# Eight conditioning vectors: row sums by VectorE with a 32x32 transpose, then selection matmuls for a group of vectors

## The chip, the core and the metric

The kernel runs on one core of one Trainium2 chip. The core has a matrix engine (TensorE, PE in the profile, with its weight loads as PEld), a vector engine (VectorE, DVE), a scalar engine (ScalarE, ACT), GpSimd (POOL) and SyncE (SP), which here only starts DMA transfers. Each engine works through its own instructions in order and waits for the others by semaphores. All of them read and write SBUF, 128 partitions wide; TensorE writes its results to PSUM. The metric is the time of one launch on the device in microseconds (us), lower is better.

## The reference

The program is a two-layer encoder trunk over 1024 tokens of width 1024, all in f32. Layer 0 has a short gated convolution and an MLP with squared ReLU (width 4096); then one shared key and value side is computed; layer 1 has latent attention with 8 heads and a second MLP. Each norm is followed by a shift and a scale which come from one conditioning vector c:

```python
mod = silu(c) @ ada_w[l] + ada_b[l]                  # 1024 -> 6 * 1024
sh_m, sc_m, g_m, sh_f, sc_f, g_f = split(mod, 6)
h = rmsnorm(x, g) * (1 + sc) + sh                    # and the like for the shared side, with kv_ada_w
```

So for each of these vectors 1024 numbers are wanted, and each is a sum over the 1024 rows of a 1024x1024 block of `ada_w`. Eight of them are wanted as columns ("feature major": the feature on the partition, 128 features x 8 columns), and they are what the change is about.

## The kernel before, in words

Almost all of the time goes into large matrix products. Each f32 factor is split into a high and a low part of a reduced format, `split_w` (L162): ScalarE writes the high part (L163), VectorE the difference (L164). `mm` (L156) then issues three matmuls for each product (L160). The larger products are done by a scheme with seven products for eight, so that VectorE also forms sums of operands.

**The vectors.** `ada_acc` (L171) computes one vector up to its last sum. It holds `acc`, 128x1024, in one buffer. For each of eight blocks k of 128 rows, SP loads 512 KB of weights into `raw` (one of four buffers, started at L115), and VectorE adds the block, multiplied row by row with silu(c): L188 for the first, L190 for the others. After eight blocks `acc[p, f]` holds 128 partial sums for each feature f, one on each partition, and they still have to be added over the partitions. `ada_fm` (L198) does this for the vectors that are wanted as columns: its `end` issues eight matmuls (L208), in each of which a 128x128 block of `acc` is the weight and a column of ones the right side, so that 128 features come out as one column. VectorE then adds the bias (L210) and, for a scale, adds one and multiplies with the norm's gain (L212, L213). `ada_bc` (L218) does something like it for vectors that are wanted on every partition (L233); it is not changed.

**Where the vectors are computed.** Both functions return lists of ten steps: the start, eight blocks, the end. The steps are appended to one list `bg`, and `run_bg(n)` (L241) takes n of them from its front at fixed places between the large products. In the conv phase that is three at a time after each pair of products, nine times, and then whatever is left (L987, L996). In the down projection of layer 0 (`down_pairs`) it is one or two with each block of weights (L709) and the rest at the end (L717). In attention it is five with each head (L1361). So the vectors s0f and h0f (the MLP of layer 0) are computed in the conv phase; s1m, h1m, skv and hkv (layer 1 and the shared side) in the down projection; s1f and h1f (the MLP of layer 1) in attention.

**What sets the order.** The instructions are put into the engines' queues by a scheduler, which goes by its own costs and by which buffers are free; only regions marked `pinned` keep the order of the program. Tiles of one tag share a fixed number of buffers, and pools are given places in SBUF one after another. Where two pools share the same space, the first use of the second waits for the last use of the first. `up` (the operands of the pairs in the conv phase, `uphi` and `uplo`) and the pools of the conv projection before it are such pools.

Of the kernel before, what the change touches and what calls it, by code (L numbers as in the profile page):

```python
# [8 lines left out]
F32 = mybir.dt.float32  # L9
# [3 lines left out]
ALU = mybir.AluOpType  # L13
AX = mybir.AxisListType
# [3 lines left out]
P = 128  # L18
D = 1024
S = 1024  # L20
KD = D // P
# [18 lines left out]
RMS = math.sqrt(D)  # L40
# [9 lines left out]
def trunk_kernel(ctx: ExitStack, tc: tile.TileContext, x, c, ada_w, ada_b, norm_g, conv_in_w, conv_w,  # L50
                 conv_b, conv_out_w, kv_ada_w, kv_ada_b, kv_norm_g, kv_a_w, kv_a_norm_g, kv_b_w,
                 q_a_w, q_a_norm_g, q_b_w, attn_o_w, mlp_up_w, mlp_down_w, consts, out):
    nc = tc.nc
    uid = [0]

    def nm(s):
        uid[0] += 1
        return f"{s}_{uid[0]}"

    def pool(name, side="left", **kw):  # L60
        return tc.alloc_tile_pool(name=name, bufs=1, side=side, reuse_waits="tile", **kw)

    cp = pool("cp")
    rawp = pool("rawp")
    ad = pool("ad")
# [25 lines left out]
    def raw_tile():  # L91
        return rawp.tile([P, D], F32, tag="raw", name=nm("raw"), bufs=4)
# [4 lines left out]
    def row_tile():  # L97
        return yp.tile([P, D], F32, tag="y", name=nm("y"), bufs=NT)
# [15 lines left out]
    def ld(out_, in_):  # L114
        nc.sync.dma_start(out_, in_)  # L115
# [3 lines left out]
    ident = cs[:, C_ID:C_ID + P]  # L119
# [21 lines left out]
    ones = cp.tile([P, P], F32, name="ones")  # L141
# [5 lines left out]
    vecs = cp.tile([P, VEC_ROWS], F32, name="vecs")  # L147
    bias = cp.tile([P, BIAS_ROWS], F32, name="bias")

    def gain(l, v):  # L150
        return vecs[:, (l * 4 + v) * 8:(l * 4 + v) * 8 + 8]

    V_CW, V_CB, V_KV, V_QA, V_KA = 64, 88, 96, 104, 107
# [17 lines left out]
    def ada_acc(accp, w, col, bias_row=None):  # L171

        acc = accp.tile([P, D], F32, tag="acc", name=nm("acc"), bufs=1)
        raws = {}
        if bias_row is not None:
            nc.gpsimd.memset(acc, 0.0)
            ld(acc[0:1, :], bias_row)

        def load(k):
            raws[k] = raw_tile()  # L180
            ld(raws[k], w[k * P:(k + 1) * P, col:col + D])

        def one(k):
            if k + 1 < KD:
                load(k + 1)
            raw, s = raws[k], csil[:, k:k + 1]
            if k == 0 and bias_row is None:
                nc.vector.tensor_scalar(acc, raw, s, None, op0=ALU.mult)  # L188
            else:
                nc.vector.scalar_tensor_tensor(acc, raw, s, acc, op0=ALU.mult, op1=ALU.add)  # L190

        load(0)
        return acc, [lambda k=k: one(k) for k in range(KD)]

    vtile = {}
    spare = [mm_ps]

    def ada_fm(accp, key, w, col, brow, g=None):  # L198

        st = {}  # L200

        def begin():
            st["acc"], st["t"] = ada_acc(accp, w, col)

        def end():
            p_ = spare[0]()
            for k in range(KD):
                nc.tensor.matmul(p_[:, k:k + 1], st["acc"][:, k * P:(k + 1) * P], ones[:, 0:1], start=True, stop=True)  # L208
            v = cp.tile([P, KD], F32, name=nm("v"))
            nc.vector.tensor_tensor(v, p_[:, :KD], bias[:, brow:brow + KD], op=ALU.add)  # L210
            if g is not None:
                nc.vector.tensor_scalar(v, v, 1.0, RMS, op0=ALU.add, op1=ALU.mult)  # L212
                nc.vector.tensor_tensor(v, v, g, op=ALU.mult)  # L213
            vtile[key] = v

        return [begin] + [lambda k=k: st["t"][k]() for k in range(KD)] + [end]

    def ada_bc(accp, key, w, col, brow, grow):  # L218

        st = {}  # L220

        def begin():
            v = accp.tile([P, D], F32, tag="gmb", name=nm("gmb"), bufs=1)
            ld(v, grow.partition_broadcast(P))
            st["v"] = v
            st["acc"], st["t"] = ada_acc(accp, w, col, brow)

        def end():
            v = st["v"]
            for n in range(2):  # L230
                sl = slice(n * HALF, (n + 1) * HALF)
                p_ = mm_ps()
                nc.tensor.matmul(p_, ones, st["acc"][:, sl], start=True, stop=True)  # L233
                nc.vector.scalar_tensor_tensor(v[:, sl], p_, RMS, v[:, sl], op0=ALU.mult, op1=ALU.mult)
            vtile[key] = v

        return [begin] + [lambda k=k: st["t"][k]() for k in range(KD)] + [end]

    bg = []
# [153 lines left out]
    def h_steps(tp, ys, half, key, dst):  # L393

        hi, lo = dst
        s1, sh = vtile["s" + key], vtile["h" + key]
        tts = {}

        def step(k):
            p_ = tp_ps()  # L400
            for t in range(4):
                nc.tensor.transpose(p_[:, t * P:(t + 1) * P], ys[half * 4 + t][:, k * P:(k + 1) * P], ident)
            tt = tp.tile([P, HALF], F32, tag="tt", name=nm("tt"), bufs=2)
            nc.scalar.activation(tt, p_, AF.Identity, scale=s1[:, k:k + 1], bias=sh[:, k:k + 1])
            tts[k] = tt

        def split(k):
            nc.vector.tensor_copy(hi[:, k, :], tts[k])
            nc.vector.tensor_tensor(lo[:, k, :], tts[k], hi[:, k, :].bitcast(F32), op=ALU.subtract)

        return [(lambda k=k: step(k), lambda k=k: split(k)) for k in range(KD)]
# [355 lines left out]
    w0, w1 = ada_w[0], ada_w[1]  # L767
# [233 lines left out]
    nx = pool("nx", "right")  # L1001
    ar = []
    bg += ada_bc(ad, "g0m", w0, 2 * D, ada_b[0:1, 2 * D:3 * D], norm_g[0, 1:2, :])
    bg += ada_fm(ad, "s0f", w0, 4 * D, 32, gain(0, 2))
    bg += ada_fm(ad, "h0f", w0, 3 * D, 24)
    conv_phase()

    def down_phase(slots, sizes, wd, src_fn, g, xsrc, xdst, next_w, key, ys=None, pairs=True):
# [82 lines left out]
    bg += ada_bc(ad, "g0f", w0, 5 * D, ada_b[0:1, 5 * D:6 * D], norm_g[0, 3:4, :])  # L1091
    last = mlp_up(0, up, hs, firsts, 2)
    ys = [row_tile() for _ in range(NT)]
    bg += ada_fm(ad, "s1m", w1, 1 * D, 48 + 8, gain(1, 0))
    bg += ada_fm(ad, "h1m", w1, 0 * D, 48)
    bg += ada_fm(ad, "skv", kv_ada_w, D, 96 + 8, vecs[:, V_KV:V_KV + 8])
    bg += ada_fm(ad, "hkv", kv_ada_w, 0, 96)
    ar, slots = down_pairs(ys, mlp_down_w[0], last)
    banks(False)
    up, ws, hs, firsts, ys = down_phase(slots, (2, 2, 4), mlp_down_w[0], from_dram(hd), "g0f", xs[0], xs[1], q_a_w[0], "1m", ys=ys,  # L1100
# [83 lines left out]
    steps = h_steps(tp, ys, 0, "kv", hk[0])  # L1184
# [3 lines left out]
    steps = h_steps(tp, ys, 1, "kv", hk[1])  # L1188
# [18 lines left out]
    ld(stab, consts[:, C_T + S:])  # L1207
    at = pool("at", "right")
    bg += ada_bc(ad, "g1m", w1, 2 * D, ada_b[1:2, 2 * D:3 * D], norm_g[1, 1:2, :])
    bg += ada_fm(ad, "s1f", w1, 4 * D, 48 + 32, gain(1, 2))  # L1210
    bg += ada_fm(ad, "h1f", w1, 3 * D, 48 + 24)

    def part(pl, tag, bufs, shape):
        return tuple(pl.tile(shape, F32R, tag=tag + "hl"[i], name=nm(tag), bufs=bufs) for i in range(2))
# [277 lines left out]
```

## Time and profile before

| what | value |
|---|---|
| median of 3 runs | 2186.09 us (2185.59 to 2193.38) |
| the profiled execution's span | 2186.4 us |
| TensorE busy | 2101.2 us (96%) |
| VectorE busy | 1523.9 us (70%) |
| ScalarE busy | 1052.9 us (48%) |
| GpSimd busy | 4.0 us |
| granted TensorE clock, mean | 0.991 |

The profile shows one execution; no other time is given for it than its span, from the first to the last instruction. A row of a timeline begins with the start and the duration in us, then the engine, the line of the kernel, the operation, the output and inputs by name, the shapes and how many instructions the row holds; in brackets stands how long the engine had been idle before and what released it. A group row has the busy time and the mean duration in ns behind the first bar, and the idle time before it with its releaser behind the second. A row of waits has us in total, how often, and the longest. A row of windows has the busy time of each engine in that stretch, then the granted TensorE clock, the share of DMA and GB/s.

### The profile page before, as it was taken

What the parts mean: (1) busy time and instruction counts of PE and PEld (TensorE: products, weight loads), DVE (VectorE), ACT (ScalarE), POOL (GpSimd) and SP (SyncE); (2) the same over time, 40 slices, a digit from 0 to 9 for tenths busy, and PEclk for the clock granted to TensorE, in tenths of its full rate; (3) what the DMA queues carried; (4) which work ended last, traced back from release to release, by engine and by line L of the source; (5) the groups of instructions that cost most, each with busy time, mean ns of one, the idle gap of its engine ahead of it and who ended that gap; (6) DMA issues with size and microseconds to landing.
All of it is one profiled execution on the core that took longest, in us unless ns stands there. A gap on an engine that the chain in (4) does not pass through costs nothing.

```text
span 2186.4 us, 25316 instructions
## 1 busy us (share of the span) xinstructions
PE 2101.2 (96%) x9702; PEld 1728.0 (79%) x9702; DVE 1523.9 (70%) x2001; ACT 1052.9 (48%) x1501; POOL 4.0 (0%) x8
## 2 busy tenths in 40 slices
PE   4999999899999999999899999999899999999998
PEld 3778888678888788888777888878688887888886
DVE  6777766876565679776788776665865655566665
ACT  4533354744454444344665555564645444444422
POOL 0000000000000000000000000000000000000000
PEclk9999999999999999999999999999999999999999
DMA  7435464256443985554224231053254544853343
GB/s 226 132 119 152 130 205 139 78 166 194 155 159 117 339 291 189 167 170 143 77 63 125 68 112 44 30 171 128 66 171 155 179 165 149 301 174 97 123 137 116
DMA packets 233551, 323.61 MB, mean 148 GB/s; under 512 B 18165, under 2 KB 141394, under 8 KB 233430
## 3 DMA queue, kind: packets, MB, share of 16 engines
q1 hardware_dynamic: 198424, 244.11, 35.8%
q10 hardware_dynamic: 35006, 77.89, 9.4%
q8 instruction: 76, 1.25, 0.3%
q14 instruction: 45, 0.37, 0.1%
HBM read 244.35 MB, written 77.59 MB: 147 GB/s over the span
## 4 chain that ended last, share of the span: by engine, by line
PE 78%; DVE 12%; ACT 6%; DMA 2%; issue 2%; ACTq 0%; SPq 0%; DVEq 0%
PE one L160 39%; PE mm L160 19%; PE big L160 9%; PE tp L160 6%; ACT junk L249 2%; PE big L1285 2%; DVE y L306 2%; DVE raw L307 2%; PE tp L1311 1%; DVE y L300 1%; DVE acc L190 1%; DVE small L1288 1%; DMA raw<-in_ada_w_dram 1%; DMA aw<-in_ada_w_dram 1%; ACT small L251 1%
## 5 line engine op out<-in xcount | busy, mean ns | idle before, releaser
L160 PE MATMUL one<-slot,uphi 128*128 128x512 f32 x1224 | 378.3, 390 | 0.0
L160 PE MATMUL big<-slot 128*128 128x512 f32 x1536 | 353.0, 390 | 0.5 <-DVE slot L164 0.4
L160 PEld LDWEIGHTS big<-slot 128*128 128x128 f32 x1536 | 287.7, 188 | 60.0 <-DVE slot L164 0.9
L160 PEld LDWEIGHTS one<-slot,uphi 128*128 128x128 f32 x1224 | 230.7, 188 | 48.4 <-issue 0.5
L160 PE MATMUL one<-slot,uplo 128*128 128x512 f32 x612 | 240.9, 394 | 8.1 <-ACT y L568 2.3
L164 DVE TENSOR_TENSOR uplo<-raw,uphi 128x1024 fp32r<-128x1024 f32 x127 | 153.1, 1221 | 133.9 <-ACT uphi L163 133.8
L160 PE MATMUL one<-ring,ring 128*128 128x512 f32 x864 | 197.9, 390 | 3.6 <-DVE ring L164 3.6
L163 ACT ACTIVATE ring<-w 128x1024 fp32r<-128x1024 f32 x84 | 88.9, 1059 | 225.6 <-PE tp L160 117.6
L163 ACT ACTIVATE uphi<-raw 128x1024 fp32r<-128x1024 f32 x127 | 134.5, 1061 | 121.6 <-PE one L160 89.1
L160 PEld LDWEIGHTS one<-ring,ring 128*128 128x128 f32 x864 | 161.7, 188 | 38.7 <-ACT ring L163 3.1
L160 PE MATMUL mm<-slot,uphi 128*128 128x512 f32 x520 | 166.6, 401 | 9.5 <-DVE slot L367 9.3
L164 DVE TENSOR_TENSOR ring<-w,ring 128x1024 fp32r<-128x1024 f32 x84 | 102.7, 1222 | 87.9 <-ACT ring L163 86.1
L160 PEld LDWEIGHTS one<-slot,uplo 128*128 128x128 f32 x612 | 115.5, 189 | 35.4 <-ACT y L493 3.3
L160 PE MATMUL mm<-ring,ring 128*128 128x512 f32 x576 | 139.5, 390 | 0.0
L160 PE MATMUL tp<-ring,ring 128*128 128x512 f32 x576 | 138.7, 389 | 0.0
L190 DVE SCALAR_TENSOR_TENSOR acc<-raw,csil,acc 128x1024 f32<-128x1024 f32 x88 | 112.8, 1282 | 32.3 <-DMA raw<-in_ada_w_dram 30.0
L160 PEld LDWEIGHTS mm<-ring,ring 128*128 128x128 f32 x576 | 107.6, 188 | 23.5 <-issue 0.8
L160 PEld LDWEIGHTS tp<-ring,ring 128*128 128x128 f32 x576 | 108.1, 188 | 22.4
L160 PEld LDWEIGHTS mm<-slot,uphi 128*128 128x128 f32 x520 | 98.9, 192 | 32.8 <-DVE slot L367 10.8
L493 ACT ACTIVATE y<-one 128x512 f32<-128x512 f32 x66 | 39.0, 591 | 163.4 <-PE one L160 102.2
L160 PE MATMUL one<-slot,s 128*128 128x512 f32 x468 | 112.6, 389 | 0.0
L164 DVE TENSOR_TENSOR ring<-raw,ring 128x1024 fp32r<-128x1024 f32 x84 | 102.4, 1219 | 11.8 <-ACT ring L163 11.8
(255 smaller groups left out, 3515.8 us busy)
## 6 DMA issues: line engine op xcount, KB each, us to landing
ha<-y ACTq DMA_DIRECT2D x168, 256.0 KB, 4.2
raw<-ha SPq DMA_DIRECT2D x84, 512.0 KB, 4.1
raw<-in_ada_w_dram SPq DMA_DIRECT2D x80, 512.0 KB, 3.9
raw<-in_mlp_up_w_dram SPq DMA_DIRECT2D x70, 512.0 KB, 4.2
w<-in_mlp_down_w_dram SPq DMA_DIRECT2D x48, 512.0 KB, 6.3
raw<-hd SPq DMA_DIRECT2D x32, 512.0 KB, 4.4
hd<-y ACTq DMA_DIRECT2D x24, 512.0 KB, 3.7
xs<-raw ACTq DMA_DIRECT2D x24, 512.0 KB, 3.0
```

What stands on the lines that cost most here:

```text
L160: nc.tensor.matmul(out_, lhs[a], rhs[b], start=first and i == 0, stop=last and i == 2, skip_group_check=more)
L163: nc.scalar.activation(hi, src, AF.Copy)
L164: nc.vector.tensor_tensor(lo, src, hi.bitcast(F32), op=ALU.subtract)
L190: nc.vector.scalar_tensor_tensor(acc, raw, s, acc, op0=ALU.mult, op1=ALU.add)
L249: nc.scalar.activation(junk, src, AF.Square, accum_out=ss)
L251: nc.scalar.activation(rt, ss, AF.Sqrt, bias=eps_d)
L300: nc.vector.tensor_tensor(y, y, p_, op=ALU.add)
L306: nc.vector.scalar_tensor_tensor(y, y, rroot(ss), self.gmb, op0=ALU.mult, op1=ALU.mult)
L307: nc.vector.tensor_tensor(xr, xr, y, op=ALU.add)
L493: nc.scalar.activation(dst, x_, AF.Copy)
L1285: nc.tensor.matmul(o_, a, m_, start=j == 0, stop=j == 4 and b * HALF + w < n)
L1288: nc.vector.tensor_reduce(mx, sp[:, :n], AX.X, ALU.max, negate=True)
```

## The change

VectorE adds over 32 columns where TensorE added over all 128 rows. `reduce` reads `acc`, 128x1024, as 32 blocks of 32 columns. With `apply_transpose` each 32x32 square (32 partitions by 32 columns) is transposed and then summed, so that `part[p, i, b]` holds, for the partition 32g + r, the sum over the 32 partitions of quadrant g of feature 32b + r. What is left is to add the four quadrants and to bring the 32 features of each block to their place among 128. Both are done by a matmul with a 0/1 matrix `sel`: `sel[:, b, :]` puts row r of each quadrant into row 32b + r. Four such matmuls, one for each b, accumulate in PSUM, and one set of four serves all vectors of a group: 16 columns for the two vectors of the conv phase, 32 for the four of the down projection, 16 for the two of attention. The operations on the bias and the gain are the same as before, but those of a group now come together.

`sel` is made once, by GpSimd, as a step of the list `bg`. A vector still has ten steps (the last is now the sum), and each group has one step more, its `end`; with `selectors` the list of the conv phase is two steps longer, the other two lists are one longer. The last part of the diff lowers the space that is kept in each partition for the descriptors of dynamic DMAs from 16384 bytes to 256; the new tiles take 3200 bytes of it.

```diff
--- before.py
+++ after.py
@@ -195,25 +195,53 @@
     vtile = {}
     spare = [mm_ps]
 
-    def ada_fm(accp, key, w, col, brow, g=None):
-
-        st = {}
-
-        def begin():
-            st["acc"], st["t"] = ada_acc(accp, w, col)
+    sel = cp.tile([P, 4, P], F32, name="sel")
+
+    def selectors():
+
+        stacked = cp.tile([P, 32], F32, name="stacked")
+        nc.gpsimd.memset(sel, 0.0)
+        nc.gpsimd.tensor_copy(stacked, ident[:, 0:32])
+        for g in range(1, 4):
+            nc.gpsimd.tensor_tensor(stacked, stacked, ident[:, 32 * g:32 * g + 32], op=ALU.add)
+        for b in range(4):
+            nc.gpsimd.tensor_copy(sel[:, b, 32 * b:32 * b + 32], stacked)
+
+    def ada_fm(accp, vectors):
+
+        n = len(vectors)
+        part = cp.tile([P, n, 32], F32, name=nm("part"))
+        steps = []
+
+        def one(i, key, w, col, brow, g):
+            st = {}
+
+            def begin():
+                st["acc"], st["t"] = ada_acc(accp, w, col)
+
+            def reduce():
+                nc.vector.tensor_reduce(part[:, i, :], st["acc"].rearrange("p (b i) -> p b i", i=32), AX.X, ALU.add,
+                                        apply_transpose=True)
+
+            steps.extend([begin] + [lambda k=k: st["t"][k]() for k in range(KD)] + [reduce])
 
         def end():
             p_ = spare[0]()
-            for k in range(KD):
-                nc.tensor.matmul(p_[:, k:k + 1], st["acc"][:, k * P:(k + 1) * P], ones[:, 0:1], start=True, stop=True)
-            v = cp.tile([P, KD], F32, name=nm("v"))
-            nc.vector.tensor_tensor(v, p_[:, :KD], bias[:, brow:brow + KD], op=ALU.add)
-            if g is not None:
-                nc.vector.tensor_scalar(v, v, 1.0, RMS, op0=ALU.add, op1=ALU.mult)
-                nc.vector.tensor_tensor(v, v, g, op=ALU.mult)
-            vtile[key] = v
-
-        return [begin] + [lambda k=k: st["t"][k]() for k in range(KD)] + [end]
+            blocks = part.rearrange("p v (k b) -> p b v k", b=4)
+            for b in range(4):
+                nc.tensor.matmul(p_[:, :n * KD].rearrange("p (v k) -> p v k", k=KD), sel[:, b, :], blocks[:, b], start=b == 0,
+                                 stop=b == 3)
+            for i, (key, w, col, brow, g) in enumerate(vectors):
+                v = cp.tile([P, KD], F32, name=nm("v"))
+                nc.vector.tensor_tensor(v, p_[:, i * KD:(i + 1) * KD], bias[:, brow:brow + KD], op=ALU.add)
+                if g is not None:
+                    nc.vector.tensor_scalar(v, v, 1.0, RMS, op0=ALU.add, op1=ALU.mult)
+                    nc.vector.tensor_tensor(v, v, g, op=ALU.mult)
+                vtile[key] = v
+
+        for i, vector in enumerate(vectors):
+            one(i, *vector)
+        return steps + [end]
 
     def ada_bc(accp, key, w, col, brow, grow):
 
@@ -1001,8 +1029,8 @@
     nx = pool("nx", "right")
     ar = []
     bg += ada_bc(ad, "g0m", w0, 2 * D, ada_b[0:1, 2 * D:3 * D], norm_g[0, 1:2, :])
-    bg += ada_fm(ad, "s0f", w0, 4 * D, 32, gain(0, 2))
-    bg += ada_fm(ad, "h0f", w0, 3 * D, 24)
+    bg.append(selectors)
+    bg += ada_fm(ad, [("s0f", w0, 4 * D, 32, gain(0, 2)), ("h0f", w0, 3 * D, 24, None)])
     conv_phase()
 
     def down_phase(slots, sizes, wd, src_fn, g, xsrc, xdst, next_w, key, ys=None, pairs=True):
@@ -1091,10 +1119,8 @@
     bg += ada_bc(ad, "g0f", w0, 5 * D, ada_b[0:1, 5 * D:6 * D], norm_g[0, 3:4, :])
     last = mlp_up(0, up, hs, firsts, 2)
     ys = [row_tile() for _ in range(NT)]
-    bg += ada_fm(ad, "s1m", w1, 1 * D, 48 + 8, gain(1, 0))
-    bg += ada_fm(ad, "h1m", w1, 0 * D, 48)
-    bg += ada_fm(ad, "skv", kv_ada_w, D, 96 + 8, vecs[:, V_KV:V_KV + 8])
-    bg += ada_fm(ad, "hkv", kv_ada_w, 0, 96)
+    bg += ada_fm(ad, [("s1m", w1, 1 * D, 48 + 8, gain(1, 0)), ("h1m", w1, 0 * D, 48, None),
+                      ("skv", kv_ada_w, D, 96 + 8, vecs[:, V_KV:V_KV + 8]), ("hkv", kv_ada_w, 0, 96, None)])
     ar, slots = down_pairs(ys, mlp_down_w[0], last)
     banks(False)
     up, ws, hs, firsts, ys = down_phase(slots, (2, 2, 4), mlp_down_w[0], from_dram(hd), "g0f", xs[0], xs[1], q_a_w[0], "1m", ys=ys,
@@ -1207,8 +1233,7 @@
     ld(stab, consts[:, C_T + S:])
     at = pool("at", "right")
     bg += ada_bc(ad, "g1m", w1, 2 * D, ada_b[1:2, 2 * D:3 * D], norm_g[1, 1:2, :])
-    bg += ada_fm(ad, "s1f", w1, 4 * D, 48 + 32, gain(1, 2))
-    bg += ada_fm(ad, "h1f", w1, 3 * D, 48 + 24)
+    bg += ada_fm(ad, [("s1f", w1, 4 * D, 48 + 32, gain(1, 2)), ("h1f", w1, 3 * D, 48 + 24, None)])
 
     def part(pl, tag, bufs, shape):
         return tuple(pl.tile(shape, F32R, tag=tag + "hl"[i], name=nm(tag), bufs=bufs) for i in range(2))
@@ -1476,7 +1501,7 @@
     from concourse import mybir as _mybir
     from concourse.bass_utils import run_bass_kernel_spmd as _run
 
-    nc = _bacc.Bacc("TRN2", target_bir_lowering=False, num_devices=1)
+    nc = _bacc.Bacc("TRN2", target_bir_lowering=False, num_devices=1, dynamic_dma_scratch_size=256)
     arrays, args = {}, []
     for name in _INS + ["consts"]:
         a = _consts() if name == "consts" else _np.ascontiguousarray(inputs[name])
```

Three places show what the scheduler made of it (the numbers in the names and the line numbers are shifted a little in the new program). The first is ScalarE's queue in the conv phase, before: `uphi_1051` is the high part of the first weights of the pairs, `w_950` and `w_974` are splits of conv weights, L895 makes operands of the pairs, L870 and L871 evict the last conv products from PSUM.

```order
L163 ACTIVATE w_950<-w_948 128x384 [waits DMAHW2_49,Activation_49]
L895 ACTIVATE slot_776<-raw_567 128x512 [waits DVE_49]
L895 ACTIVATE q_998<-y_996 128x512 [waits DVE_49]
L163 ACTIVATE w_974<-w_972 128x384 [waits DMAHW3_49,PE_49,Activation_49]
L895 ACTIVATE b_997<-y_996 128x512
L870 ACTIVATE y_1030<-mm_782 128x512 [waits PE_49]
L871 ACTIVATE y_1029<-mm_781 128x512 [waits PE_49]
L870 ACTIVATE y_1030<-one_779 128x512 [waits PE_49]
L871 ACTIVATE y_1029<-one_778 128x512 [waits PE_49]
L163 ACTIVATE uphi_1051<-raw_1045 128x1024 [waits DMAHW6_49,DVE_49,PE_49]
```

And the same queue of the new program, where `uphi_1053` is that split and L923 and L898 are the lines L895 and L870:

```order
L163 ACTIVATE w_850<-w_848 128x384 [waits DMAHW5_49,PE_49,Activation_49]
L163 ACTIVATE uphi_1053<-raw_1047 128x1024 [waits DMAHW6_49]
L923 ACTIVATE slot_777<-raw_449 128x512 [waits DVE_49]
L923 ACTIVATE slot_778<-raw_449 128x512 [waits DVE_49]
L923 ACTIVATE slot_777<-raw_509 128x512 [waits DVE_49]
```

The split has moved up behind the conv weights `w_850`, 21 places, and waits for its DMA alone; before, it stood behind the last evictions and also waited for VectorE and TensorE.

The second place is VectorE's queue at the end of the conv phase, before. `s_352` is the low part of an operand that TensorE's next product reads.

```order
L190 SCALAR_TENSOR_TENSOR acc_1943<-raw_2211,csil,acc_1943 128x1024 [waits DMAHW2_49,DVE_49]
L506 TENSOR_TENSOR y_2050<-y_2050,one_2075 128x512 [waits Activation_49]
L190 SCALAR_TENSOR_TENSOR acc_1943<-raw_2271,csil,acc_1943 128x1024 [waits DMAHW3_49,DVE_49]
L965 TENSOR_TENSOR y_1977<-one_1978,y_1836 128x512 [waits PE_49]
L164 TENSOR_TENSOR uplo_2166<-raw_2104,uphi_2165 128x1024 [waits Activation_49]
L446 TENSOR_TENSOR raw_2104<-raw_2104,raw_2102 128x512 [waits DVE_49]
L484 TENSOR_TENSOR y_2106<-y_2106,mm_2137 128x512 [waits PE_49]
L449 TENSOR_TENSOR raw_2102<-raw_2102,raw_2104 128x512 [waits DVE_49]
L164 TENSOR_TENSOR slot_2307<-raw_2328,slot_2307 128x1024 [waits DMAHW4_49,Activation_49]
L164 TENSOR_TENSOR s_352_2171<-raw_2104,s_351_2170 128x512 [waits Activation_49]
```

And now (L993 is the line L965):

```order
L190 SCALAR_TENSOR_TENSOR acc_2063<-raw_2208,csil,acc_2063 128x1024 [waits DMAHW1_49,DVE_49]
L534 TENSOR_TENSOR y_2047<-y_2047,one_2072 128x512 [waits Activation_49]
L190 SCALAR_TENSOR_TENSOR acc_2063<-raw_2268,csil,acc_2063 128x1024 [waits DMAHW2_49,DVE_49]
L190 SCALAR_TENSOR_TENSOR acc_2063<-raw_2271,csil,acc_2063 128x1024 [waits DMAHW3_49,DVE_49]
L223 TENSOR_REDUCE part_150<-acc_2063 128x32 [waits DVE_49]
L993 TENSOR_TENSOR y_1974<-one_1975,y_1845 128x512 [waits PE_49]
L164 TENSOR_TENSOR uplo_2163<-raw_2101,uphi_2162 128x1024 [waits Activation_49]
L512 TENSOR_TENSOR y_2103<-y_2103,mm_2134 128x512 [waits PE_49]
L474 TENSOR_TENSOR raw_2101<-raw_2101,raw_2099 128x512 [waits DVE_49]
L164 TENSOR_TENSOR slot_2308<-raw_2329,slot_2308 128x1024 [waits DMAHW4_49,Activation_49]
L477 TENSOR_TENSOR raw_2099<-raw_2099,raw_2101 128x512 [waits DVE_49]
L164 TENSOR_TENSOR s_350_2168<-raw_2101,s_349_2167 128x512 [waits Activation_49]
```

One more addition to `acc` stands here, since the list runs one step later, and behind it the sum with its transpose; then the same instructions as before follow.

The third is TensorE's queue there, before and now:

```order
L160 MATMUL one_2075<-q_998,uplo_2037 128x512
L160 MATMUL one_2075<-q_998,uphi_2036 128x512 x2
L208 MATMUL mm_2275<-ones,acc_1943 128x1 [waits DVE_49]
L208 MATMUL mm_2275<-ones,acc_1943 128x1 x7
L160 MATMUL one_2107<-slot_776,s_352_2171 128x512 [waits DVE_49]
L160 MATMUL one_2107<-slot_776,s_351_2170 128x512 [waits Activation_49]
```

```order
L160 MATMUL one_2072<-q_1000,uplo_2034 128x512
L160 MATMUL one_2072<-q_1000,uphi_2033 128x512 x2
L232 MATMUL mm_2276<-part_150,sel 128x16 [waits DVE_49,Pool_49]
L232 MATMUL mm_2276<-part_150,sel 128x16 [waits Pool_49] x3
L160 MATMUL one_2104<-slot_778,s_350_2168 128x512 [waits DVE_49]
L160 MATMUL one_2104<-slot_778,s_349_2167 128x512 [waits Activation_49]
```

The selection matmuls of the group stand at the very place where the eight matmuls of its second vector stood; the group of the first vector, further up, is gone.

## The prediction

> **What bounds the kernel now.** I read the page first: busy shares, the 40 slices and the chain.
>
> ```profile
> span 2186.4 us, 25316 instructions
> PE 2101.2 (96%) x9702; PEld 1728.0 (79%) x9702; DVE 1523.9 (70%) x2001; ACT 1052.9 (48%) x1501; POOL 4.0 (0%) x8
> PE   4999999899999999999899999999899999999998
> ...
> DVE  6777766876565679776788776665865655566665
> ...
> PE 78%; DVE 12%; ACT 6%; DMA 2%; issue 2%; ACTq 0%; SPq 0%; DVEq 0%
> ```
>
> PE works for 2101.2 of 2186.4 us. Only the first slice is far from full, and the chain of waits lies on PE for 78%. So a matmul that goes is worth its whole time wherever PE has no gap, and what VectorE does costs nothing unless it comes late for PE. The span is 2186.4 us, the median of the runs 2186.1, so a difference worked out against the span carries over to the median less 0.3 us.
>
> Next the view of the line that the change removes, L208, with the engine that waited for it, and PE's timeline around one of its eight groups.
>
> ```profile
> L208 PE MATMUL mm<-ones,acc x80: 164/250/250, 245.9 to 1338.3; 128*128 128x1 f32 x80
> L208 PE MATMUL one<-ones,acc x48: 164/250/250, 784.7 to 917.5; 128*128 128x1 f32 x48
> DVE v L210: 10.9, 7
> ```
>
> ```profile
> 784.75 1.84 PE L208 MATMUL one<-ones,acc 128*128 128x1 f32 x16
> 786.45 3.03 PE L160 MATMUL mm<-ring,ring 128*128 128x512 f32 x12
> 789.31 2.88 PE L160 MATMUL tp<-ring,ring 128*128 128x512 f32 x12
> 792.03 2.88 PE L160 MATMUL mm<-ring,ring 128*128 128x512 f32 x12
> ```
>
> The 128 records are 64 matmuls, two passes for each f32 matmul, 16 passes in a group. The group starts at 784.75 and the next work at 786.45: 1.70 us, or 0.106 us a pass, for one column of output. Twelve matmuls of the ring follow each other in 2.72 us (789.31 to 792.03), but the first twelve after the group took 2.86 (786.45 to 789.31), so it also costs 0.14 us of pipeline. **One vector costs 1.84 us of PE**, with nothing else able to run there.
>
> Windows then tell how much slack the other engines have where the groups stand.
>
> ```profile
> core 0: us, PE busy (x) PEld busy (x) DVE busy (x) ACT busy (x) POOL busy (x), PEclk, DMA share, GB/s
> 110.00:150.00 40.00, 37.79 (x160) 30.76 (x159) 27.04 (x32) 15.55 (x21) 0.00 (x0) 0.96 0.38 110
> 250.00:300.00 50.00, 49.31 (x226) 40.78 (x225) 37.51 (x42) 19.09 (x23) 0.00 (x0) 1.00 0.58 182
> 750.00:800.00 50.00, 50.00 (x230) 41.65 (x230) 37.54 (x36) 21.52 (x25) 0.00 (x0) 1.00 0.82 282
> 800.00:850.00 50.00, 50.00 (x230) 41.68 (x229) 45.07 (x41) 19.77 (x22) 0.00 (x0) 1.00 0.76 253
> 850.00:900.00 50.00, 49.96 (x228) 41.11 (x227) 45.89 (x50) 18.98 (x22) 0.00 (x0) 1.00 0.55 178
> 1300.00:1350.00 50.00, 49.47 (x300) 43.37 (x299) 35.63 (x63) 27.77 (x54) 0.00 (x0) 1.00 0.20 67
> ```
>
> PE is full in all of them but the first, where 2.21 us are lost to a stall and (1 − 0.96) × 40 = 1.6 us to a lower granted clock. VectorE is near its own limit from 800 to 900 us.
>
> **Removed: eight groups.** 8 × 1.84 = 14.7 us of PE, two of them in the conv phase, four in the down projection of layer 0 (784.75 and three more up to 917.5), two in attention, where PE is full to 1%.
>
> **Added on PE: three groups of four selection matmuls.** Eight passes a group, of 16 or 32 columns. The trace has passes of one column at 0.106 us and f32 passes of 512 columns, below.
>
> ```profile
> L233 PE MATMUL mm<-acc,ones 128*128 128x512 f32 x16 | 7.8, 598 | 0.0
> L1288 DVE TENSOR_REDUCE small<-big 128x1 f32<-128x1024 f32 x8 | 9.8, 1223 | 3.2 <-PE big L1286 2.8
> L190 DVE SCALAR_TENSOR_TENSOR acc<-raw,csil,acc 128x1024 f32<-128x1024 f32 x88 | 112.8, 1282 | 32.3 <-DMA raw<-in_ada_w_dram 30.0
> L176 POOL MEMSET acc<- 128x1024 f32 x4 | 3.8, 956 | 1545.5 <-DVE lat L1133 734.0 <-DVE uplo L164 712.1 <-DMA raw<-in_ada_w_dram 99.4
> ```
>
> So a group lies between 8 × 0.106 + 0.14 = 1.0 us and 8 × 0.598 + 0.14 = 4.9 us. Sixteen or 32 columns are far nearer to one than to 512, though the right side is read at a stride of four elements; I take 1.0, and 3.0 us for the three. The upper end would be 14.7, the whole saving.
>
> **Added on VectorE: eight sums of 128x1024 into 128x32 with the transpose.** A plain sum of as many elements takes 1.223 us (L1288, from PSUM and with one output a row). With a transpose there is no row. Below I bound it by the plain 1.2, above by one pass for the sum and seven more of the kind, some 10 us; I take 1.22, since an instruction that reads 1024 elements a row takes 1.2 to 1.3 us in both rows here whatever it does with them. Eight are 9.8 us, hidden under PE's matmuls where VectorE has slack. On the other side VectorE no longer stands behind PE for each vector:
>
> ```profile
> DVE v L210 <- PE one L208: 7.8, 3, 4.8
> DVE v L210 <- PE mm L208: 2.3, 1, 2.3
> ```
>
> These are the waits from 735 to 960 us: 10.1 us of VectorE standing idle in its own order, until PE reached a group. The change puts 4 × 1.22 = 4.9 us of sums in that stretch and takes most of the 10.1 out, so I cost it at nothing there; without that cover it would be 4.9. [...]
>
> **Added on POOL: the selection matrix.** One memset of 128x512, half of a 956 ns row, five copies and three additions of small blocks, at the start. POOL's first work of before waits until 99.4 us for a DMA, and PE needs the matrix only just ahead of 284.79 us (quoted further down). Nothing; what it could disturb is VectorE in the first slice, where PE is only four tenths busy; 0 to 2 us, within the range.
>
> **Moved: the stall at the first pair.** The smaller reserve for DMA descriptors frees 12.9 KB of each partition after the new tiles, and in the new order ScalarE's split of the first pair's weights waits for its load alone and stands some 20 rows earlier; in the old order it stands behind the evictions of the conv projection.
>
> ```profile
> 83.57 0.37 SPq L115 DMA_DIRECT2D raw<-in_conv_in_w_dram  x1
> ```
>
> ```profile
> 86.99 0.63 ACT L895 ACTIVATE slot<-raw 128x512 fp32r<-128x512 f32 x1 [1.29 <-DVE raw L894]
> ...
> 115.80 0.69 DVE L872 TENSOR_TENSOR y<-one,y 128x512 f32<-128x512 f32 x1 [5.49 <-PE one L160]
> ...
> 117.58 1.05 ACT L163 ACTIVATE uphi<-raw 128x1024 fp32r<-128x1024 f32 x1
> ...
> 118.66 1.23 DVE L164 TENSOR_TENSOR uplo<-raw,uphi 128x1024 fp32r<-128x1024 f32 x1
> ...
> 119.94 0.50 PE L160 MATMUL one<-slot,uplo 128*128 128x512 f32 x1 [2.21 <-DVE uplo L164]
> ```
>
> PE waits 2.21 us for uplo. In the new order its first pair waits only for L872's eviction, which ends at 116.49, before PE is done at 119.94 − 2.21 = 117.73. The new place has a wait of its own: the load leaves at 83.57, and ScalarE, which now comes to the split some 1.3 us ahead of the L895 row, holds everything behind it until the load is in, some 2 or 3 us. Behind it stand operands of the pairs, wanted from 117.73 on, and conv weights that are split several blocks ahead; no PE row between 84 and 117 us waits for ScalarE, so I put nothing for it. What is late next is nothing that I can see, so the stall and its slow clock go: 3.8 us. [...]
>
> **Moved: one step later in the background list.** The matrix takes a step, so each later load and sum comes one place later, and at the end of the conv phase five steps are left over, not three. In VectorE's order the last two additions, the sum, L965, uplo and six more then stand ahead of s, which PE waits for.
>
> ```profile
> 272.75 1.28 DVE L190 SCALAR_TENSOR_TENSOR acc<-raw,csil,acc 128x1024 f32<-128x1024 f32 x1 [0.77 <-DMA raw<-in_ada_w_dram]
> 275.24 1.28 DVE L190 SCALAR_TENSOR_TENSOR acc<-raw,csil,acc 128x1024 f32<-128x1024 f32 x1 [0.61 <-DMA raw<-in_ada_w_dram]
> 277.85 0.69 DVE L965 TENSOR_TENSOR y<-one,y 128x512 f32<-128x512 f32 x1 [1.33 <-PE one L160]
> 279.00 1.23 DVE L164 TENSOR_TENSOR uplo<-raw,uphi 128x1024 fp32r<-128x1024 f32 x1 [0.45 <-ACT uphi L163]
> 283.20 0.68 DVE L164 TENSOR_TENSOR s<-raw,s 128x512 fp32r<-128x512 f32 x1
> 283.31 0.33 SPq L115 DMA_DIRECT2D raw<-in_conv_out_w_dram  x1
> 284.79 3.03 PE L160 MATMUL one<-slot,s 128*128 128x512 f32 x12
> 293.95 0.50 PE L160 MATMUL one<-slot,uplo 128*128 128x512 f32 x1 [0.69 <-ACT y L493]
> ```
>
> The additions wait for their loads, 2.5 us apart (272.75, 275.24). A fifth comes at about 277.8, ends at 279.0, the sum ends at 280.3. L965 starts 2.4 us later than before and uplo 1.8 later, as 0.6 of its idle time takes up the rest; s ends at 283.88 + 1.8 = 285.7. PE, with a group of 1.0 in place of 1.84, is there at 284.79 − 0.84 = 283.95: **a stall of 1.7 us**. At 0.69 us of idle (293.95) the window keeps clock 1.00, at 2.21 it fell; 1.7 is nearer to the second, so I add the 1.6 of that window and take 3.3 (ends 0 and 3.9, the latter with a load 0.6 later). The load for the MLP that now stands ahead of the second conv_out load waits for the sum, at 280.3, before that load's 283.31: nothing.
>
> **Sum:** −14.7 + 3.0 − 3.8 + 3.3 = −12.2 us, 2186.4 − 12.2 = **2174 us**.
>
> **The rivals.** *VectorE sets the pace where the matmuls go* (chance 0.32): from 800 to 900 us it has 4 to 5 us free in 50, and in attention its results come just in time. If the six groups there gain nothing (6 × 1.84 − 2 × 1.0 = 9.0 lost), 2174.2 + 9.0 = 2183 us; a part of it, or the stall at 119.94 staying (2178), falls into the same class. For it speaks VectorE's 45.89 of 50; against it PE's 50.00 beside it and the 10.1 us handed back. *The transposing sum is slow and makes it slower* (0.11): its place is VectorE's queue, where everything for PE stands behind it. Let x be what one costs over 1.22 us. The one at the end of the conv phase and the two in attention are then paid in full, 3x, and the four in the down projection beyond the 12.5 + 4.9 + 4.1 = 21.5 us that the windows show free, 4x − 21.5. The gain is gone from 3x = 12.2, a sum of 5.3 us; at 10 us (x = 8.8) it costs 26.4 + 13.7, so 2174.2 + 40.1 = 2214 us. Only the lack of a row speaks for it. [...] *The change does not do what it says*: selection matmuls at the upper end, 2174.2 + 11.7 = 2186 us (in the 0.32).
>
> **How the numbers follow.** The forecast has 0.57. About 0.5% is what a measurement of this kernel can tell from no change, 10.9 us, so faster means under 2175.2: my value lies 1 us below. It holds if the conv end costs no more than 4.3 us; without that stall it would be 2170.9, and some 4 us of VectorE's returned time in attention would bring 2167. Range 2167 to 2185, which takes in the first rival and leaves out the second. The slow sum ends above 2197 us but for 0.01 of its 0.11, so: faster 0.57, same 0.33, slower 0.10.
>
> **What would show it.** In the new profile: selection groups of some 1.0 us each, start to next work; sums near 1.22 us; no wait of PE for uplo near 118 us and a clock of 1.00 in that window; a wait for s of 1 to 2 us near 280; PE's busy time lower by about 13 us. I am wrong if the sums take over 2 us, if PE shows new waits for VectorE's ring between 780 and 920 us, or if the first stage, up to 84 us, has become longer.

## The result and the profile after

The changed kernel takes 2190.62 us in the median of 21 runs, beside 2187.39 us for the kernel before in as many: a ratio of 1.0014 with a 95% interval of 1.0007 to 1.0020. It is 3 us slower where I had forecast 12 us less, and outside my range. The profiled execution has a span of 2186.8 us and took 2188.6; the time of a run is its span and 1.8 us.

Everything that I had worked out from the profile can be found in the new one, so the lines that answer to those of the prediction come first. The page, and the row of windows where the stall at the first pair was:

```profile
span 2186.8 us, 25133 instructions
PE 2101.1 (96%) x9598; PEld 1715.8 (78%) x9598; DVE 1531.7 (70%) x2009; ACT 1053.8 (48%) x1501; POOL 6.2 (0%) x17
...
PE 77%; DVE 13%; ACT 6%; DMA 2%; issue 2%; ACTq 0%; SPq 0%; DVEq 0%
```

```profile
110.00:150.00 40.00, 40.00 (x176) 32.66 (x175) 26.90 (x30) 13.46 (x19) 0.00 (x0) 1.00 0.45 139
250.00:300.00 50.00, 46.89 (x202) 37.99 (x201) 38.63 (x47) 18.94 (x22) 0.00 (x0) 0.97 0.53 171
850.00:900.00 50.00, 50.00 (x221) 40.88 (x220) 49.21 (x49) 19.80 (x22) 0.00 (x0) 1.00 0.54 177
```

From 110 to 150 us PE is full and the clock is at 1.00: the stall is gone. From 250 to 300 us there is the new one, with the clock at 0.97. The new operations, from the views of their lines, and a selection group of the down projection on PE's timeline:

```profile
L223 DVE TRANSPOSE_TENSOR_REDUCE part<-acc x8: 1233/1242/1245, 232.9 to 1280.0; 128x32 f32<-128x1024 f32 x8
L232 PE MATMUL mm<-part,sel x16: 188/262/283, 278.2 to 1377.7; 128*128 128x16 f32 x16
L232 PE MATMUL one<-part,sel x8: 219/283/284, 919.4 to 920.1; 128*128 128x32 f32 x8
```

```profile
919.41 0.98 PE L232 MATMUL one<-part,sel 128*128 128x32 f32 x8
920.22 3.00 PE L160 MATMUL mm<-ring,ring 128*128 128x512 f32 x12
923.05 2.88 PE L160 MATMUL tp<-ring,ring 128*128 128x512 f32 x12
```

A sum with its transpose takes 1.24 us. A group takes 0.81 us to the next work and 0.11 more behind it, since the first twelve matmuls then take 2.83 us (920.22 to 923.05) and not 2.72: 0.92 us.

And yet PE's busy time is the same to 0.1 us, 2101.1 for 2101.2, with 104 records fewer. Hence what remains must have become slower. I matched the matmuls of the two traces one by one (those of the vectors left out) and took the difference of their starts, after less before:

```
start in the kernel before, us   after - before, us
 115.5                            -1.2
 140.5                            -5.0    the stall at the first pair
 241.1                            -3.7    conv pairs: gives 1.4 back
 266.3                            -5.2    the first group
 291.5                            -1.7    the new stall before s
 442.1                            -0.8
 718.6                            +3.3    up projection of layer 0: gives 4.1 back
 768.9                            +3.7
 919.8                            -3.8    the four groups of the down projection
1121.2                            -4.5
1347.4                            -6.3    attention
1598.6                            -3.5
1875.2                            +0.1    up projection of layer 1: gives 3.7 back
2151.9                            +0.3
```

The larger steps down are those that I had forecast. The 0.7 us up to 1121.2 are not: the granted clock of the kernel before is 0.50 from 1087 to 1090 us, the changed kernel has no such stretch there, and that outweighs its new group. Of the steps up, the new stall was forecast. Three others, 9.2 us together, lie in the stretches in which pairs are computed with `slot`, `q` or `b` as one operand and `uphi` or `uplo` as the other. In these the loss is no wait: it grows evenly, by about 0.35 us in 25. The last one, 2.8 us in attention up to 1598.6, is of another kind; it is taken up again at the end of the part on the prediction. The windows from 550 to 650 us, of before and of after, with the columns PE, PEld, DVE, ACT, POOL, and then the granted clock:

```profile
550.00:650.00 100.00, 100.00 (x439) 82.12 (x438) 59.50 (x82) 49.70 (x62) 0.00 (x0) 1.00 0.45 152
```

```profile
550.00:650.00 100.00, 100.00 (x433) 81.06 (x432) 58.19 (x80) 49.98 (x62) 0.00 (x0) 1.00 0.44 149
```

PE is busy for all of it in both, at clock 1.00 in both, and does 439 matmuls in one and 433 in the other. Neither PE's busy share nor the clock shows the loss. The count does, and so does the busy time of the weight loads (PEld), which falls with it from 82.12 to 81.06 us. The view of the tile `q` between 450 and 740 us (shortest, median and longest duration in ns), before and after:

```profile
L160 PE MATMUL one<-q,uphi x120: 389/389/393, 455.4 to 716.1; 128*128 128x512 f32 x120
L160 PE MATMUL one<-q,uplo x60: 389/389/389, 455.1 to 715.6; 128*128 128x512 f32 x60
```

```profile
L160 PE MATMUL one<-q,uphi x120: 387/395/404, 455.0 to 719.3; 128*128 128x512 f32 x120
L160 PE MATMUL one<-q,uplo x60: 387/392/398, 454.8 to 718.9; 128*128 128x512 f32 x60
```

The same matmuls of the same tiles have become longer and uneven. In a single one it is a few ns; there are thousands.

### The profile page after: what moved, and what is told of

Read it like the earlier page. It is cut to its first block, busy times and chain, and to the rows that moved or that the text cites. A ratio compares the mean times of both kernels' runs of the same rounds, so it can differ in the third digit from the quotient of the medians.

```text
span 2186.8 us, 25133 instructions
## 1 busy us (share of the span) xinstructions
PE 2101.1 (96%) x9598; PEld 1715.8 (78%) x9598; DVE 1531.7 (70%) x2009; ACT 1053.8 (48%) x1501; POOL 6.2 (0%) x17
## 4 chain that ended last, share of the span: by engine, by line
PE 77%; DVE 13%; ACT 6%; DMA 2%; issue 2%; ACTq 0%; SPq 0%; DVEq 0%
PE one L160 39%; PE mm L160 18%; PE big L160 9%; PE tp L160 6%; ACT junk L277 2%; PE big L1310 2%; DVE y L334 2%; DVE raw L335 2%; DMA raw<-in_ada_w_dram 1%; PE tp L1336 1%; DVE acc L190 1%; DVE y L328 1%; DVE small L1313 1%; ACT small L279 1%; ACT z L1168 1%
## 5 line engine op out<-in xcount | busy, mean ns | idle before, releaser
L160 PE MATMUL mm<-slot,uplo 128*128 128x512 f32 x260 | 106.1, 408 | 4.2 <-ACT slot L392 2.2
```

The lines of the kernel that those rows point to most:

```text
L160: nc.tensor.matmul(out_, lhs[a], rhs[b], start=first and i == 0, stop=last and i == 2, skip_group_check=more)
```

## What the slower matmuls have in common

What the change moves without touching it is where the tiles lie in SBUF. Pools are allocated from both ends. The low ones (`rawp`, `yp`, `arB`, `arC`, `wr`) stand behind `cp`, the pool of constants and the first one; the high ones (`arA`, `cA`, `cB`, `up`, `sd`) are counted from the top. In the kernel before, every one of these pools starts at 224 modulo 256 bytes of its partition. The change takes 16384 − 256 = 16128 = 63 × 256 bytes away from below `cp` and adds 2048 (`sel`) + 128 (`stacked`) + 1024 (`part`) bytes to it, 12.5 × 256. So the low pools now start at 96 modulo 256 and the high ones still at 224. The kernel before has a line for this that I had read over: `cp.tile([P, 8], F32, name="even")` (L117), a tile of 32 bytes that nothing uses.

With the tiles' addresses from the built programs set beside the trace, each f32r matmul of 512 columns falls into one of two classes, by whether its moving operand and its weights start at the same remainder modulo 256 (even, in what follows) or not (uneven). The spacing is from start to start, where a matmul of the same class follows within 245 ns:

```
kernel   remainders differ by   matmuls   mean spacing, ns
before     0                      8267      227.2
after      0                      6155      227.6
after    128                      2112      232.8
```

It is not the remainder 96 itself: from 300 to 400 us of the changed kernel, the matmuls with both operands in `arB` at 96 have a spacing of 227.3. 2112 × (232.8 − 227.2) = 11.8 us, about what is missing.

The borders between pools tell which two remainders have to be compared. Take the 125 spacings from a matmul with both operands in `arA` (remainder 224) to one with both in `arB` (96), or back. Each matmul is even in itself, but the columns that the first one reads and the weights of the second are 128 apart. They take 232.8 and 232.5 ns in the changed kernel, 226.9 and 226.8 at the same places of the kernel before. In 58 spacings from `arA` with `up` to `arB` with `up` it is the other way round: the second matmul is uneven in itself, but its weights and the columns of the first are even. They take 226.7 ns (226.9 before). So what counts here is the moving operand of the running matmul against the weights of the next one. The first few spacings behind an uneven one are longer too: for `arA` with `up` 231.5, 232.2 and 230.5 ns, and 226.8 from the fourth on.

Up to here that is a correlation in one pair of traces; the experiments take it apart.

## The experiments

**e1, the changed kernel with its pools even again.** Theory A is the one above. Rival B blames the smaller reserve for the descriptors, rival C the new work on VectorE and GpSimd.

```diff
-    cp.tile([P, 8], F32, name="even")
+    cp.tile([P, 40], F32, name="even")
```

> The changed kernel with the unused tile `even` 160 bytes long in place of 32, so that all pools that are allocated from the low end move up by 128 bytes; no instruction and no place in a queue changes. Theory A (remainders): a matmul whose moving operand and whose weights start at addresses that differ by 128 modulo 256 takes 232.8 ns from start to start, not 227.2; the changed kernel has 2112 such matmuls, this one none. So 2112 x 5.6 ns = 11.8 us go: ratio to before about 1.0014 - 0.0054 = 0.996, and all matmuls in the up projections at about 227 ns. Rival B (the smaller reserve for descriptors slows the loads) and rival C (the sums, the transposes or the selection matrix slow TensorE): nothing changes, ratio 1.0014.

Measured: 2181.36 us, ratio 0.9970 (0.9959 to 0.9982), 0.0044 or 9.6 us under the changed kernel. The profiled spans differ by 10.6 us (2186.8 and 2176.2). The 8267 matmuls are all in one class at 227.1 ns, and `q` has its old durations:

```profile
L160 PE MATMUL one<-q,uphi x120: 389/389/397, 452.7 to 713.4; 128*128 128x512 f32 x120
L160 PE MATMUL one<-q,uplo x60: 389/389/389, 452.5 to 713.0; 128*128 128x512 f32 x60
```

The instructions of this kernel stand in the same order on every engine as those of the changed one. B and C fall as the cause of the slower matmuls: all that they name is still in it. The two traces have the same 9598 matmul records, so the difference up to the last one, 11.0 us, can be split by place. The uneven spacings lose 10.4 us and the even ones, mostly right behind them, 2.7; elsewhere the changed kernel is 2.1 us ahead, 1.1 of them because PE waits for s for 3.5 us in e1 and for 2.4 in the changed kernel.

**e2, the other way round: the kernel before with the same 128 bytes.** The edit is that of e1, made in the kernel before.

> The kernel before with `even` 160 bytes long in place of 32, nothing else; the same queues. It has 2112 matmuls with operands 128 bytes apart modulo 256. Theory A: 11.8 us slower, ratio 1.0054, with a mean of 232.8 ns for these matmuls. Rivals B and C: nothing of their causes is in it, ratio 1.000.

Measured: 2197.18 us, ratio 1.0045 (1.0030 to 1.0059), 9.8 us slower, with 2112 matmuls at 232.8 ns. Its windows from 550 to 650 us have the changed kernel's count, 433, again at clock 1.00:

```profile
550.00:650.00 100.00, 100.00 (x433) 80.98 (x432) 57.79 (x80) 49.97 (x63) 0.00 (x0) 1.00 0.43 148
```

So 128 bytes of an unused tile, and nothing else, cost what the change had lost. The 11.8 us of the product lie within the interval of this run, 6.6 to 12.9 us.

**e3, the kernel before with the smaller reserve alone.**

```diff
-    nc = _bacc.Bacc("TRN2", target_bir_lowering=False, num_devices=1)
+    nc = _bacc.Bacc("TRN2", target_bir_lowering=False, num_devices=1, dynamic_dma_scratch_size=256)
```

> The kernel before with 256 bytes for descriptors in place of 16384 and nothing else; the pools move down by 63 x 256 bytes, so no operands stand 128 bytes apart. Theory A: the wait for uplo at 118 us and the slower clock after it go, -3.8 us, ratio 0.9983. Rival B: 12 us or more slower in the up projections, ratio 1.004 or above. Rival C: 0.9983, as A.

Measured: 2183.45 us, ratio 0.9984 (0.9975 to 0.9994), 3.5 us faster. From 110 to 150 us PE is full:

```profile
110.00:150.00 40.00, 40.00 (x178) 33.13 (x177) 28.40 (x31) 14.68 (x19) 0.00 (x0) 1.00 0.47 145
```

This is the term of the stall without the rest of the change: the room, and not the sums, moves ScalarE's split forward (it starts at 86.54 us here, 117.58 before). The 3.5 us also hold whatever else the room moves, in attention for one, as will be seen. B falls a second time.

**e4, the matrix made at once, out of the list.** On top of e1:

```diff
-    bg.append(selectors)
+    selectors()
```

> The kernel of the first run (pools 128 bytes up), with the selection matrix made in the program's text right away and not as a step of the background list, so that the steps stand where they stood before. Theory A with the wait of 2.4 us for s at 281 us and the slow clock after it (1.7 us) as its second part: these go too, 4.1 us below the first run, ratio about 0.994. If the place in the list is not what makes s late: as the first run, 0.996.

Measured: 2176.22 us, ratio 0.9951 (0.9938 to 0.9963). That is 5.1 us under e1 by the medians and 4.2 by the ratios, whose intervals just overlap. PE's waits from 84 to 300 us, in e1 and then in e4:

```profile
PE one L160 <- DVE s L164: 3.5, 1, 3.5
PE one L160 <- ACT y L521: 0.7, 1, 0.7
```

```profile
PE one L160 <- ACT y L521: 0.7, 1, 0.7
PE one L160 <- DVE slot L871: 0.4, 1, 0.4
```

The wait for s is gone with the one step that stood too many in the list. Between the traces of e1 and e4 the step at this place is 5.25 us: 3.5 of waiting, the rest right behind it, where the changed kernel has a granted clock of 0.51 (281.5 to 285.0 us). The profiled executions as wholes do not show it (spans of 2176.2 and 2177.1), since e4's has losses that e1's has not: granted clocks of 0.57 from 71 to 75 and from 1078 to 1082 us, where e1 has 1.00, and 3.0 us of PE's waits for VectorE's `ring` from 735 to 960 us, where e1 has 1.8. By the median this kernel is, with e6, the best of all here, some 11 us under the one before.

**e5, other distances.** The changed kernel with `even` 96 and 64 bytes long:

> The changed kernel with `even` 96 bytes long: the low pools stand 64 bytes off the high ones modulo 256 in place of 128, with the same queues. If the cost is one of 128 byte halves, the 2112 matmuls cost as much as at 128 (232.8 ns) or as little as at 0 (227.2); if it grows with the distance, about 230; if any unequal remainder costs the same, 232.8.

> The same with `even` 64 bytes long: low pools 96 bytes off (160 the other way round). By halves 232.8 or 227.2 as the run at 64 bytes shows, by distance between that run and 128, by any unequal remainder 232.8.

One run each, 2191.2 and 2197.7 us, which says little by itself. The spacings say more:

```
kernel          remainders differ by   matmuls   mean spacing, ns
e5, 96 bytes      0                      6155      227.9
e5, 96 bytes     64 / 192            288 / 1824    230.2 / 233.3
e5, 64 bytes      0                      6155      227.9
e5, 64 bytes     96 / 160            288 / 1824    234.0 / 233.6
```

It does not grow evenly with the distance, and it is not a matter of halves of 128 bytes: differences of 96, 160 and 192 cost about as much as 128. The one of 64 costs less where it was tried. Its 230.2 rests on 150 spacings, 119 of them in the conv projection, and those take 228.2 ns in the kernel before, 229.7 at 64, 232.4 at 128 and 234.0 at 96. In the kernel before, low and high pools differ by 256 modulo 512 (`arB` starts at 78560, `arA` at 157664), and its spacing is 227.2 ns.

**e6, each sum twice.** On e4, to see whether the sums are hidden:

```diff
             def reduce():
+                nc.vector.tensor_reduce(twice[:, 0, :], st["acc"].rearrange("p (b i) -> p b i", i=32), AX.X, ALU.add,
+                                        apply_transpose=True)
                 nc.vector.tensor_reduce(part[:, i, :], ...
```

> The kernel of e4 with each of the eight sums done twice, the first time into a tile that nobody reads: 8 x 1.24 = 9.9 us more on VectorE and nothing else. If the sums are hidden: as e4, within 2 us (ratio 0.995), the 1 us at the end of the conv phase, where one sum just fitted the idle time, among them. If VectorE sets the pace where the groups went: up to 9.9 us slower, ratio 0.9995, with PE waiting for the ring between 780 and 930 us.

Measured: a median of 2176.19 us beside e4's 2176.22; the ratio of 0.9965 (0.9951 to 0.9978) is against other runs of the kernel before, which were 1.2 us faster in the median than those beside e4, and its interval overlaps e4's. 9.9 us more of VectorE cost nothing that can be measured. Where VectorE is fullest, from 850 to 900 us, it was busy for 48.44 of 50 us, and PE lost 0.69 there. Its waits for VectorE's `ring` from 735 to 960 us, 2.1 us, are no longer than e4's 3.0:

```profile
850.00:900.00 50.00, 49.31 (x216) 40.23 (x216) 48.44 (x49) 18.18 (x18) 0.00 (x0) 1.00 0.54 179
```

**e7, every vector its own group.** On e4, with `ada_fm` called for one vector at a time and `end` in the step of the sum:

```diff
-            steps.extend([begin] + [lambda k=k: st["t"][k]() for k in range(KD)] + [reduce])
+            steps.extend([begin] + [lambda k=k: st["t"][k]() for k in range(KD)] + [lambda: (reduce(), end())])
...
-        return steps + [end]
+        return steps
...
-    bg += ada_fm(ad, [("s0f", w0, 4 * D, 32, gain(0, 2)), ("h0f", w0, 3 * D, 24, None)])
+    bg += ada_fm(ad, [("s0f", w0, 4 * D, 32, gain(0, 2))])
+    bg += ada_fm(ad, [("h0f", w0, 3 * D, 24, None)])
```

> The kernel of e4 with each vector a group of its own, its four selection matmuls and its operations on the bias right behind its sum, where the old groups stood: eight groups in place of three. 5 x 1.0 = 5 us more on PE and nothing else: ratio 0.995 + 0.0023 = 0.997. If the waits of VectorE for each group, which come back, cost something too: 2 us more or above, 0.998 and more.

Measured: 2180.32 us, ratio 0.9971 (0.9959 to 0.9982), 4.1 us above e4 by the medians; the intervals overlap a little. In the matched traces of e4 and e7 the starts step up by 0.81 us at each of the five added groups, 4.1 together. Of VectorE's waits for groups, 10.1 us from 735 to 960 us in the kernel before, 3.9 come back. That these cost nothing fits the numbers, but it is not shown.

## Why the prediction was wrong

**The step that failed** is "Moved: the stall at the first pair". There I took the 12.9 KB of room in each partition as a gain alone. The same number, taken modulo 256, is the loss: 12928 bytes are 50.5 × 256, and the half puts 2112 matmuls on operands with unequal remainders, 9.6 to 9.8 us by e1 and e2. My sum had no term for it, and none of my rivals named it; that nothing much would change I had held possible, but from other causes. The profile of before could not show the cost, since all its operands are even. But the shift could be worked out from the diff, and the tile `even` stood in the code.

The other steps, in their order:

- *Removed, 1.84 us a vector.* Right. In the matched traces the starts step by 1.85 us at each of the four places of the down projection. That "PE is full to 1%" in attention would turn the step into time there did not hold, as the last paragraph shows.
- *Selection groups, 1.0 us.* Right: 0.92 us. The columns' stride costs nothing to be seen, and the upper end of 4.9 us was far off.
- *Sums, 1.22 us and hidden.* Right: 1.24 us, and e6 shows them hidden even when doubled. The rival of the slow transpose falls. The one of VectorE that sets the pace stays small in the down projection: with 49.21 of 50 us busy it still kept PE at 50.00, and PE's waits for `ring` from 735 to 960 us are 1.3 us before and 1.7 after.
- *VectorE's waits, 10.1 us.* They are gone: no wait for a group's result is left among VectorE's waits from 735 to 960 us. Whether they had cost anything stays open.
- *The stall at the first pair, −3.8 us.* Right: −3.84 us in the matched traces, and 3.5 us by e3. The early split waits for its load as I had said, 1.66 us at the head of ScalarE's queue, and PE does not wait for it; from 84 to 300 us it waits for s and 0.7 us for `y`, for nothing else:

```profile
85.58 1.06 ACT L163 ACTIVATE uphi<-raw 128x1024 fp32r<-128x1024 f32 x1 [1.66 <-DMA raw<-in_conv_in_w_dram]
```

- *The wait for s, +3.3 us with the clock.* The mechanism was right, the size a little low (the 0.6 us of idle time ahead of uplo is 0.45 in the row, which makes 0.15 of it). In the changed kernel:

```profile
273.68 1.28 DVE L190 SCALAR_TENSOR_TENSOR acc<-raw,csil,acc 128x1024 f32<-128x1024 f32 x1 [1.73 <-DMA raw<-in_ada_w_dram]
275.00 1.25 DVE L223 TRANSPOSE_TENSOR_REDUCE part<-acc 128x32 f32<-128x1024 f32 x1
```

```profile
281.54 4.57 PE L160 MATMUL one<-slot,s 128*128 128x512 f32 x12 [2.42 <-DVE s L164]
285.95 0.40 PE L160 MATMUL one<-b,uplo 128*128 128x512 f32 x1
```

The last addition still waits 1.73 us for its load, the sum follows it, and PE waits 2.42 us for s instead of 1.7. Then its twelve matmuls take 4.41 us (281.54 to 285.95) for 2.72: another 1.7 of slower clock (granted clock 0.51 from 281.5 to 285.0 us), as the row of 0.96 had it before, and as I had added it. Here the clock fell after a wait of 2.42 us. In e1 the same place cost 5.25 us.

With the pools even (e1) the kernel came out 6.6 us under the one before, at a ratio whose interval reaches from 3.9 to 9.0 us, and 10 us in the profiled executions (spans of 2186.4 and 2176.2). My sum was 12.2. 2 us of the difference are the wait for s, larger in e1 than I had put it. Another part is attention, where I had put two groups less and one new one at 2.7 us: in the matched traces of the kernel before and e1 the difference goes from −10.4 at 1120 us to −10.1 at 1600, so nothing of it is left. PE waits longer there. Its waits from 1120 to 1600 us add up to 19.5 us before, 23.2 in the changed kernel, 23.4 in e1, and 22.2 in e3, which has the old groups and only the smaller reserve. One of the longest new ones is for `v`, in the changed kernel and in e3 alike; the kernel before has none for it:

```profile
PE mm L160 <- DVE v L1294: 1.6, 1, 1.6
```

```profile
PE mm L160 <- DVE v L1269: 1.6, 1, 1.6
```

So most of these longer waits come with the room as well, a second price of the step that I had taken as a gain alone. On the other side e1's profiled execution gains what I had not forecast, 0.8 us up to 110 us and 1.6 where the kernel before has its half clock at 1087; that the 10 us come so near to 12.2 is in part luck.

## What to carry to other kernels

A change that adds or removes a tile near the start of the allocation moves every pool behind it. Work out the shift modulo 256 bytes for pools that are counted from opposite ends, and set it right with a tile that nobody uses; here 128 bytes decided between 0.14% slower and 0.30% faster. Compare the count of matmuls in a window in which PE is full: here it was 433 for 439 in 100 us, while PE's busy share (100.00 of 100 us) and the clock (1.00) did not show the loss. Room that comes free is not a gain alone: it changes the order in places that the change does not touch. And a step that is added to a list from which work is taken in fixed portions moves everything behind it; set up constants outside it.

## What the runs showed of the hardware

An f32r matmul of 512 columns followed the one ahead of it in 227 to 228 ns (227.2 in the kernel before, 227.1 in e1, 227.6 and 227.9 in the changed kernel and in e5) when the moving operand of the running one and the weights of the next one start at the same remainder modulo 256 bytes within the partition. It followed in 232.8 to 234.0 ns when the remainders differ by 96, 128, 160 or 192 (234.0, 232.8, 233.6 and 233.3), and in 230.2 when they differ by 64, which was seen in few places. With a difference of 256 bytes, as between the low and the high pools of the kernel before, it was 227.2. The trace shows the running matmul and the load of the next one's weights at the same time. In the kernel before, the second of the two matmuls of the first row starts at about 560.35 us, and so does the load of the next one's weights:

```profile
560.12 0.62 PE L160 MATMUL one<-slot,uphi 128*128 128x512 f32 x2
560.57 0.39 PE L160 MATMUL one<-slot,uplo 128*128 128x512 f32 x1
```

```profile
560.35 0.19 PEld L160 LDWEIGHTS one<-slot,uplo 128*128 128x128 f32 x1
```

Why unequal remainders should make them slower stays open, since no run here separates the two reads.
